# Second layer's up-projections: seven block products for eight on 20 of 22 pairs of hidden tiles

## The chip, the cores and the metric

The kernel runs on one core of a Trainium2 chip. The metric is device time in microseconds (us) of one execution, as the median of several runs. The engines are TensorE (PE in the profile; PEld is its weight load), VectorE (DVE), ScalarE (ACT), GpSimd (POOL) and SyncE (SP), which issues most transfers. Each engine works through its own list of instructions in a fixed order.

## The reference

Two layers of a hybrid backbone (neighbourhood attention and mLSTM in the first, latent attention in the second). What matters here is the gated feed-forward part, which both layers end in, in the second layer on 512 tokens:

```python
def conv_ffn(h, w_up, conv_w, conv_b, w_down):
    u = dwconv_centred(h @ w_up, conv_w, conv_b)
    a, g = jnp.split(u, 2, axis=-1)
    return (a * jax.nn.silu(g)) @ w_down
```

`h` is 512 x 1024, `w_up` 1024 x 5632 and `w_down` 2816 x 1024. The convolution has width 3 along the tokens. All is fp32, and the kernel holds fp32 accuracy by splitting each operand into a high and a low part (type fp32r) and taking three products: high x high, high x low, low x high.

## The kernel before

**Layout.** Activations lie as features x tokens: 8 blocks (k) of 128 features, 512 columns. The 2816 hidden features are 22 tiles of 128 (j). Each tile needs a pair of up-projection tiles: g = 0 is the value half, g = 1 the gate half. One up tile is 8 k x 3 products = 24 matmuls of 512 columns into one half of a two-bank PSUM tile `pu` (`proj`, L181).

**Weights.** `wload` (L175) fetches 128 x 1024 floats into `wraw` (a ring of two buffers), ScalarE copies the high part (`whi`), VectorE subtracts to get the low part (`wlo`). All of these small operations are recorded under the lines of the helpers: L139 matmul, L145 ScalarE, L148 two-input tensor operations, L154 VectorE's scalar-tensor-tensor.

**After the product** (`up_post`, L1214 on): ScalarE applies the middle tap and the bias of the convolution, two VectorE operations add the outer taps (straight from PSUM), ScalarE takes the SiLU of the gate, VectorE multiplies, ScalarE copies the high part of the hidden tile (`hid0`), VectorE subtracts the low part (`hid1`).

**Order.** The pairs come in groups (`plan`): here 3, 3, 3, 3, 3, 2, 1, 4. The first group is done in `front`, in two halves of 256 tokens, since the second half of `h` is finished late by the norm chain. For each further group the pairs' up-projections are written first and then, in `down`, the down-projection of the group before: 8 output tiles `pd`, each 3 matmuls per j of that group, added to `acc` by VectorE (by ScalarE copied for the first group). The last group's down-projection (`pdl`) runs in two halves of 256 tokens and feeds the last norm.

What stands in the program is the start only: a scheduler in the framework sets each engine's list, which is fixed when the kernel is built. Buffers are rings, and a writer waits until the last reader of its buffer is done.

## Time and profile before

| what | before |
|---|---|
| median of 3 runs | 1832.33 us (1832.32 to 1834.01) |
| profiled execution, its own time | 1829.64 us |
| span of the profile | 1827.5 us |
| PE busy | 1768.6 us (97%) |
| PEld / DVE / ACT / POOL busy | 1460.9 / 1162.9 / 748.5 / 254.6 us |
| granted TensorE clock, mean | 0.993 |

The feed-forward part of the second layer lies from about 1433 us to the end. Busy shares are averages over the whole program; the sections below read the stage itself. A matmul's own duration overlaps that of its neighbours, so the pace of TensorE is read from stretches: so many matmuls in so many us.

### The profile page before, as it was taken

How to read it: one execution, taken by the hardware profiler on the slowest of the kernel's cores; microseconds unless marked ns; L12 is line 12 of the kernel's file. 1: busy time of each engine (PE TensorE's matmuls, PEld its weight loads, DVE VectorE, ACT ScalarE, POOL GpSimd, SP SyncE). 2: the span in 40 equal slices, each digit the busy share in tenths (PEclk: the TensorE clock that was granted, in tenths of full speed). 3: DMA queues.
4: the chain of work that ended last, by engine and by line, in shares of the span. 5: the costliest groups of instructions: out<-in, count | busy, mean ns of one | idle time of the engine just before them, and what ended most of it. 6: DMA issues, size and time to landing. Idle time of an engine off the chain costs nothing.

```text
span 1827.5 us, 26602 instructions
## 1 busy us (share of the span) xinstructions
PE 1768.6 (97%) x10498; PEld 1460.9 (80%) x10498; DVE 1162.9 (64%) x2210; ACT 748.5 (41%) x1297; POOL 254.6 (14%) x306
## 2 busy tenths in 40 slices
PE   6999999999999999999999999899999999999997
PEld 4777787887778888888888877788878888888885
DVE  3383677557356686776764655788894574556565
ACT  3333444444444422232221334577775354333241
POOL 1000123234320000000000001344441200000000
PEclk8999999999999999999999999999999999999998
DMA  9343322214212343434421211000012132224231
GB/s 308 110 127 127 123 86 81 62 55 133 76 35 93 125 131 114 134 120 135 131 83 47 91 36 47 24 12 13 13 35 84 47 104 90 95 81 136 72 93 47
DMA packets 63261, 162.39 MB, mean 89 GB/s; under 512 B 6273, under 2 KB 19793, under 8 KB 63137
## 3 DMA queue, kind: packets, MB, share of 16 engines
q1 hardware_dynamic: 61616, 156.52, 27.0%
q0 software_dynamic: 1376, 4.04, 0.7%
q8 instruction: 83, 1.36, 0.3%
q14 instruction: 42, 0.34, 0.1%
q10 hardware_dynamic: 144, 0.13, 0.0%
HBM read 158.57 MB, written 2.10 MB: 88 GB/s over the span
## 4 chain that ended last, share of the span: by engine, by line
PE 84%; DVE 6%; POOL 2%; issue 2%; ACT 2%; DMA 1%; DVEq 0%; POOLq 0%; ACTq 0%
PE pu L139 29%; PE pd L139 13%; PE yps L139 4%; PE sp L139 4%; PE qkp L139 3%; PE puf L139 3%; PE pdl L139 3%; PE vtk L139 3%; PE qp L139 2%; PE pt L142 2%; PE ot L139 2%; PE vp L139 2%; PE kp L139 2%; PE ops L139 1%; PE ysum L390 1%
## 5 line engine op out<-in xcount | busy, mean ns | idle before, releaser
L145 ACT ACTIVATE whi<-wraw 128x1024 fp32r<-128x1024 f32 x186 | 195.2, 1058 | 484.8 <-PE pu L139 219.8
L148 DVE TENSOR_TENSOR wlo<-wraw,whi 128x1024 fp32r<-128x1024 f32 x184 | 224.7, 1226 | 236.4 <-ACT whi L145 235.8
L139 PE MATMUL pu<-h,whi 128*128 128x258 f32 (+1 forms) x1280 | 318.5, 339 | 0.0
L139 PEld LDWEIGHTS pu<-h,whi 128*128 128x128 f32 x1280 | 219.6, 188 | 28.7 <-issue 0.8
L139 PE MATMUL pd<-hid,whi 128*128 128x512 f32 (+1 forms) x864 | 233.4, 358 | 1.2 <-DVE acc L148 1.2
L139 PE MATMUL pu<-h,wlo 128*128 128x512 f32 (+1 forms) x640 | 216.6, 339 | 0.0
L139 PEld LDWEIGHTS pd<-hid,whi 128*128 128x128 f32 x864 | 152.2, 188 | 28.2 <-DVE acc L148 2.8
L148 POOL TENSOR_TENSOR ry<-rv,mhalf 128x2 f32<-128x2 f32 (+2 forms) x26 | 23.0, 884 | 1017.9 <-DVE rv L151 1017.9
L139 PE MATMUL pd<-hid,wlo 128*128 128x512 f32 (+1 forms) x432 | 153.1, 356 | 0.0
L148 DVE TENSOR_TENSOR acc<-pd,acc 128x512 f32<-128x512 f32 (+1 forms) x192 | 109.0, 585 | 47.9 <-PE pd L139 46.6
L139 PEld LDWEIGHTS pu<-h,wlo 128*128 128x128 f32 x640 | 120.9, 189 | 13.6
L139 PE MATMUL pu<-hb,whi 128*128 128x512 f32 x304 | 119.8, 394 | 0.0
L139 PE MATMUL pu<-hb,wlo 128*128 128x512 f32 x304 | 119.2, 392 | 0.0
L139 PE MATMUL pu<-lb,whi 128*128 128x512 f32 x304 | 118.0, 388 | 0.0
L154 DVE SCALAR_TENSOR_TENSOR av<-aw,s,av 128x512 f32<-128x512 f32 x140 | 102.5, 748 | 23.2 <-DMA aw<-in_ada_w_dram 22.6
L151 POOL TENSOR_SCALAR P<-P,rl 128x768 f32<-128x768 f32 (+1 forms) x96 | 85.3, 890 | 143.1 <-DVE nm L151 49.8
L139 PEld LDWEIGHTS pd<-hid,wlo 128*128 128x128 f32 x432 | 81.2, 188 | 11.9
L154 DVE SCALAR_TENSOR_TENSOR u<-pu,c_ffn_conv,u 128x769 f32<-128x769 f32 x80 | 81.1, 1014 | 10.1 <-ACT u L145 9.4
L139 PE MATMUL sp<-kr,qh 128*128 128x512 f32 (+1 forms) x256 | 71.0, 353 | 2.5 <-ACT P L145 1.3
L148 DVE TENSOR_TENSOR pTl<-pt,pTh 128x512 fp32r<-128x512 f32 x96 | 64.5, 682 | 5.7 <-ACT pTh L145 4.9
L139 PEld LDWEIGHTS pu<-hb,wlo 128*128 128x128 f32 x304 | 57.1, 188 | 13.4
L139 PEld LDWEIGHTS pu<-lb,whi 128*128 128x128 f32 x304 | 57.1, 188 | 12.7
(454 smaller groups left out, 3840.1 us busy)
## 6 DMA issues: line engine op xcount, KB each, us to landing
wraw<-in_ffn_up_dram SPq DMA_DIRECT2D x88, 512.0 KB, 3.6
aw<-in_ada_w_dram SPq DMA_DIRECT2D x112, 256.0 KB, 2.7
wraw<-in_ffn_down_dram SPq DMA_DIRECT2D x44, 512.0 KB, 3.6
aw<-in_ada_w_dram SPq DMA_DIRECT2D x40, 512.0 KB, 4.5
wraw<-in_w_in_dram SPq DMA_DIRECT2D x20, 512.0 KB, 3.7
wraw<-in_w_tok_dram SPq DMA_DIRECT2D x8, 512.0 KB, 4.2
wraw<-in_w_out_dram SPq DMA_DIRECT2D x8, 512.0 KB, 3.7
wraw<-in_w_o_dram SPq DMA_DIRECT2D x8, 512.0 KB, 3.5
```

The costliest lines, as they stand in the source:

```text
L139: PE.matmul(out=o, lhsT=l, rhs=r, start=start, stop=stop)
L142: PE.transpose(out=o, in_=i, identity=ident[0:i.shape[0], 0:i.shape[0]])
L145: S.activation(out=o, in_=i, func=func, **kw)
L148: e.tensor_tensor(out=o, in0=x, in1=y, op=op)
L151: e.tensor_scalar(out=o, in0=x, scalar1=s1, scalar2=s2, op0=op0, op1=op1)
L154: V.scalar_tensor_tensor(out=o, in0=x, scalar=s, in1=y, op0=op0, op1=op1)
L390: PE.matmul(out=ps[32 * i:32 * i + 32, 0:w], lhsT=ones32, rhs=src, start=first, stop=last, tile_position=(0, 32 * i))
```

## The change

The product of an up pair is seen as a 2 x 2 block product. The weights of a pair are four blocks: value or gate half (rows) by features k 0-3 or 4-7 (columns). The activations are four blocks: features 0-3 or 4-7 by the first or second 256 tokens. The direct way takes 8 block products, each 4 k x 3 = 12 matmuls of 256 columns; Strassen's scheme (in Winograd's form, with fewer additions) takes 7, at the price of sums: of activation blocks (T1 to T4, made once), of weight blocks (four per pair, on GpSimd) and of products.

This is done for the tiles j = 2 to 21. Per pair the new `up_s` has 7 products of 12 matmuls of 256 columns. Their results are put together in `c0`, `c1` in SBUF: ScalarE copies two of them, VectorE adds six times from PSUM, GpSimd adds once. The convolution then reads `c0`, `c1` from SBUF instead of PSUM. `weights(j)` is run one pair ahead, one step per product: it splits seven operands of 128 x 512 (w0 to w6, in `wq`, a ring of 8), with the four sums in between, made in place in `wraw`. On these pairs the gated multiply, the hidden low part and the low parts of the down weights go from VectorE to GpSimd. The groups become 2, 2, 2, 2, 1, 2, 2, 2, 2, 1, 4, so that eight down passes become eleven of fewer tiles, with the same matmuls in all. The norm chain ahead leaves `h` in fp32 in `acc` for the T sums, with one more ScalarE pass on six of eight feature blocks. The first layer is unchanged.

```diff
-                A, B, h = mod
+                A, B, h = mod[:3]
+                whole = len(mod) > 3
...
+                    elif whole:
+                        act(y(k), y(k), AF.Identity, bias=b)
+                        act(hi, y(k))
+                        tt(V, lo, y(k), fr(hi), ALU.subtract)
...
-            before_last=lambda: None, pumps=(0, 0), nst=NSF):
+            before_last=lambda: None, pumps=(0, 0), nst=NSF, blocks=None):
...
                 act(us[1], us[1], AF.Silu)
-                tt(V, us[0], us[0], us[1], ALU.mult)
+                eg = G if blocks else V
+                tt(eg, us[0], us[0], us[1], ALU.mult)
                 hi, lo = (t[:, c0:c0 + w] for t in hid[j])
                 act(hi, us[0])
-                tt(V, lo, us[0], fr(hi), ALU.subtract)
+                tt(eg, lo, us[0], fr(hi), ALU.subtract)
+            nh = n // 2
+            B, places, wst, nraw = {}, {}, {}, [0]
+            def blocks_ready(names):
+                h1_, h2_ = slice(0, nh), slice(nh, n)
+                a_ = lambda k0, c: acc[:, k0:k0 + 4, c]
+                t1, t3, t2, t4 = a_(0, h1_), a_(0, h2_), a_(4, h2_), a_(4, h1_)
+                for k0, c, nm in ((0, h1_, "11"), (4, h1_, "21"), (4, h2_, "22")):
+                    B[nm] = [lambda k, t=t, k0=k0, c=c: t[:, k0 + k, c] for t in h]
+                if "T4" in names:
+                    tt(G, t4, t4, t2, ALU.subtract)
+                else:
+                    tt(V, t1, t3, t1, ALU.subtract)
+                    tt(G, t3, t2, t3, ALU.subtract)
+                    tt(V, t2, t2, t1, ALU.subtract)
+                    places.update(blocks(fw))
+                for nm in names:
+                    t = {"T1": t1, "T2": t2, "T3": t3, "T4": t4}[nm]
+                    B[nm] = []
+                    for s in range(2):
+                        ps_ = places[nm][s]
+                        for k0, o in ps_:
+                            kn = o.shape[1]
+                            if s == 0:
+                                act(o, t[:, k0:k0 + kn])
+                            else:
+                                hi_ = [p for kk, p in places[nm][0] if kk <= k0][-1]
+                                kk_ = [kk for kk, p in places[nm][0] if kk <= k0][-1]
+                                tt(V, o, t[:, k0:k0 + kn], fr(hi_[:, k0 - kk_:k0 - kk_ + kn]), ALU.subtract)
+                        B[nm].append(lambda k, ps_=ps_: [o[:, k - k0] for k0, o in ps_
+                                                       if k0 <= k < k0 + o.shape[1]][0])
+            def block(o, w, b):
+                for k in range(4):
+                    wh, wl = (t[:, k * 128:(k + 1) * 128] for t in w)
+                    mm(o, wh, b[0](k), k == 0, False)
+                    mm(o, wh, b[1](k), False, False)
+                    mm(o, wl, b[0](k), False, k == 3)
+            def slot():
+                return fw.tile([128, 2, 512], F32R, tag="q", name="wq", bufs=8)
+            def raw_up(src):
+                nraw[0] += 1
+                p, tag = (wp, "wr") if nraw[0] % 4 < 2 else (fw, "raw")
+                raw = p.tile([128, 1024], F32, tag=tag, name="wraw", bufs=2)
+                nc.sync.dma_start(out=raw, in_=src)
+                return raw
+            def wunit(src, lo_e=None):
+                raw = raw_up(src)
+                hi, lo = (slot().rearrange("p a b -> p (a b)") for _ in range(2))
+                act(hi, raw)
+                tt(lo_e or V, lo, raw, fr(hi), ALU.subtract)
+                return hi, lo
+            def weights(j):
+                ra, rg = (raw_up(a["ffn_up"][l, 2 * j + g]) for g in range(2))
+                w = wst[j] = []
+                a11, a12, a21, a22 = ra[:, 0:512], ra[:, 512:1024], rg[:, 0:512], rg[:, 512:1024]
+                for i, r in enumerate((a11, a22, a12, a11, a21, a22, a12)):
+                    hi, lo = (lambda t: (t[:, 0], t[:, 1]))(slot())
+                    act(hi, r)
+                    tt(V, lo, r, fr(hi), ALU.subtract)
+                    w.append((hi, lo))
+                    if i == 1:
+                        tt(G, a22, a21, a22, ALU.add)
+                        tt(G, a21, a11, a21, ALU.subtract)
+                        tt(G, a11, a22, a11, ALU.subtract)
+                    elif i == 2:
+                        tt(G, a12, a12, a11, ALU.subtract)
+                    yield
+            def up_s(j, early):
+                w = wst.pop(j)
+                nxt = weights(j + 1) if j + 1 < NH else iter(())
+                C = [fw.tile([128, pw], F32, tag=f"c{g}", name=f"c{g}") for g in range(2)]
+                c11, c12, c21, c22 = (c[:, o:o + nh] for c in C for o in (0, nh))
+                us = [None, None]
+                def conv(g):
+                    u = us[g] = fw.tile([128, pw], F32, tag=f"u{g}", name=f"u{g}", bufs=1)
+                    cw = fcw[l][:, g * NH + j, :]
+                    act(u, C[g], AF.Identity, scale=cw[:, 1:2], bias=cw[:, 3:4])
+                    stt(u[:, 1:n], C[g][:, 0:n - 1], cw[:, 0:1], u[:, 1:n], ALU.mult, ALU.add)
+                    stt(u[:, 0:n - 1], C[g][:, 1:n], cw[:, 2:3], u[:, 0:n - 1], ALU.mult, ALU.add)
+                for i, (m, nm) in enumerate([(0, "11"), (1, "T4"), (2, "21"), (3, "T2"), (4, "T3"), (5, "T1"), (6, "22")]
+                                            if not early else
+                                            [(0, "11"), (2, "21"), (3, "T2"), (4, "T3"), (5, "T1"), (6, "22"), (1, "T4")]):
+                    if i % 2 == 0:
+                        pa = ps_a("pu")
+                    p = pa[:, 512 * (i % 2):512 * (i % 2) + nh]
+                    block(p, w[m], B[nm])
+                    if m == 0:
+                        act(c12, p)
+                    elif m == 1:
+                        if early:
+                            tt(V, c21, p, c21, ALU.add)
+                        else:
+                            act(c21, p)
+                    elif m == 2:
+                        tt(V, c11, p, c12, ALU.add)
+                    elif m == 3:
+                        tt(V, c12, p, c12, ALU.add)
+                    elif m == 4:
+                        if early:
+                            tt(V, c21, p, c12, ALU.add)
+                        else:
+                            tt(V, c22, p, c12, ALU.add)
+                            tt(G, c21, c21, c22, ALU.add)
+                    elif m == 5:
+                        tt(V, c22, p, c21 if early else c22, ALU.add)
+                        tt(V, c12, p, c12, ALU.add)
+                    else:
+                        tt(V, c12, p, c12, ALU.add)
+                    next(nxt, None)
+                    if m == (1 if early else 5):
+                        conv(1)
+                conv(0)
+                run(nxt)
+                gated(j, us, 0, pw)
             def up(j):
+                if blocks:
+                    return up_s(j, j == plan[1][0])
...
-                wus = {j: [wload(a["ffn_up"][l, 2 * j + g],
+                wus = {j: [wunit(a["ffn_up"][l, 2 * j + g]) if blocks and 2 * n_ + g >= 3 else
+                           wload(a["ffn_up"][l, 2 * j + g],
...
+                        if blocks and sg is parts[-1][-1]:
+                            blocks_ready(("T2", "T3", "T1"))
...
-                wu = {j: (wload(a["ffn_down"][l, j], tag="wd", pool=fw, bufs=gmax) if n_ < gmax
+                wu = {j: ((wload(a["ffn_down"][l, j], lo_e=G) if n_ < 3 else wunit(a["ffn_down"][l, j], G)) if blocks
+                          else wload(a["ffn_down"][l, j], tag="wd", pool=fw, bufs=gmax) if n_ < gmax
...
+            if blocks:
+                blocks_ready(("T4",))
+                run(weights(plan[1][0]))
...
+                    elif blocks and i == 0:
+                        for _ in range(KD // 2):
                             next(dn, None)
...
-    out_proj(a["w_o"], h1, acc1, SH, xs1, mods1["G1"], tuple(range(KD)), (mods1["A2"], mod_shift(1, 3), h1), NSO[1],
+    out_proj(a["w_o"], h1, acc1, SH, xs1, mods1["G1"], tuple(range(KD)), (mods1["A2"], mod_shift(1, 3), h1, True),
+             NSO[1],
...
-    ffn(1, SH, SH, [SH], xs1, h1, accp, acc1, mods1["G2"], [3] * 5 + [2, 1, 4], done=emit_out)
+    def blocks1(fw):
+        v = vkp.tile([128, 6, TX], F32R, tag="v1", name="tb", bufs=2).rearrange("p a b -> p (a b)")
+        f = fw.tile([128, 3, TX * 2], F32R, name="tb2", bufs=1)
+        fl = lambda t: t.rearrange("p (a b) -> p a b", a=4)
+        return {"T2": [[(0, fl(v[:, 0:1024]))], [(0, fl(v[:, 1024:2048]))]],
+                "T3": [[(0, fl(v[:, 2048:3072]))], [(0, fl(f[:, 0]))]],
+                "T1": [[(0, fl(f[:, 1]))], [(0, fl(f[:, 2]))]],
+                "T4": [[(0, hb1[:, 0:4, 256:512])], [(k, h1lo[k][:, 256:512].unsqueeze(1)) for k in range(4)]]}
+    ffn(1, SH, SH, [SH], xs1, h1, accp, acc1, mods1["G2"], [2] * 4 + [1] + [2] * 4 + [1, 4], done=emit_out,
+        blocks=blocks1)
```

**How the instructions move, 1: VectorE.** In the middle of the second layer's feed-forward part, one pair before: the outer taps from `pu`, the low parts of later weights, the multiply and the low hidden part.

```order
L154 SCALAR_TENSOR_TENSOR u0_15627<-pu_15565,fcw1_13268,u0_15627 128x511 x2
L148 TENSOR_TENSOR wlo_15732<-wraw_15729,whi_15731 128x1024
L154 SCALAR_TENSOR_TENSOR u1_15631<-pu_15596,fcw1_13268,u1_15631 128x511
L148 TENSOR_TENSOR wlo_15827<-wraw_15824,whi_15826 128x1024
L148 TENSOR_TENSOR u0_15627<-u0_15627,u1_15631 128x512
L148 TENSOR_TENSOR hid1_15636<-u0_15627,hid0_15635 128x512
```

In the change, the second pair of a group, from the fourth weight operand (w3) of the pair to come to the first tap of the value half:

```order
L148 TENSOR_TENSOR wq_14773<-wraw_14716,wq_14773 128x512
L148 TENSOR_TENSOR c0_14700<-pu_14742,c0_14700 128x256
L148 TENSOR_TENSOR c1_14701<-pu_14776,c0_14700 128x256
L148 TENSOR_TENSOR wq_14791<-wraw_14718,wq_14791 128x512
L148 TENSOR_TENSOR wq_14808<-wraw_14718,wq_14808 128x512
L148 TENSOR_TENSOR c1_14701<-pu_14776,c1_14701 128x256
L148 TENSOR_TENSOR c0_14700<-pu_14776,c0_14700 128x256
L148 TENSOR_TENSOR wq_14829<-wraw_14716,wq_14829 128x512
L154 SCALAR_TENSOR_TENSOR u1_14811<-c1_14701,fcw1_13268,u1_14811 128x511
L148 TENSOR_TENSOR c0_14700<-pu_14815,c0_14700 128x256
L148 TENSOR_TENSOR acc1_13270<-pd_14842,acc1_13270 128x512
L154 SCALAR_TENSOR_TENSOR u0_14832<-c0_14700,fcw1_13268,u0_14832 128x511
```

The taps now read two operands in SBUF, the multiply and the low hidden part are gone from this list, and the split w3 (first row) stands ahead of the additions from PSUM and of the taps.

**2: GpSimd.** Before, nothing stands between the last norm work ahead of the pairs and the first of the last norm:

```order
L151 TENSOR_SCALAR acc1_13270<-acc1_13270,mod1_102 128x256 [waits DVE_49]
L148 TENSOR_TENSOR lb2_12992<-acc1_13270,hb_12846 128x256 [waits PE_49,Activation_49]
L148 TENSOR_TENSOR lb5_13139<-acc1_13270,hb_12846 128x256 [waits PE_49,Activation_49]
L148 TENSOR_TENSOR ry_16508<-rv_16507,mhalf_90 128x2 [waits DVE_49]
L148 TENSOR_TENSOR x1_4390<-acc1_13270,x1_4390 128x256 [waits DVE_49] x2
```

In the change, from the end of a group's first pair to the start of the next group's (`wlo` are down weights; `u0` is the multiply, `hid1` the low hidden part, `wraw` the four sums, `c1` the addition of two products):

```order
L148 TENSOR_TENSOR wlo_14667<-wraw_14664,whi_14666 128x1024 [waits DMAHW2_49,PE_49,Activation_49]
L148 TENSOR_TENSOR u0_14654<-u0_14654,u1_14633 128x512 [waits DVE_49,Activation_49]
L148 TENSOR_TENSOR wlo_14673<-wraw_14670,whi_14672 128x1024 [waits DMAHW3_49,PE_49,Activation_49]
L148 TENSOR_TENSOR hid1_14659<-u0_14654,hid0_14658 128x512 [waits Activation_49]
L148 TENSOR_TENSOR wraw_14718<-wraw_14718 128x512 [waits DMAHW1_49,DVE_49]
L148 TENSOR_TENSOR wraw_14718<-wraw_14716,wraw_14718 128x512 [waits DMAHW0_49,Pool_49]
L148 TENSOR_TENSOR wraw_14716<-wraw_14718,wraw_14716 128x512 [waits Pool_49]
L148 TENSOR_TENSOR wraw_14716<-wraw_14716 128x512 [waits DVE_49,Pool_49]
L148 TENSOR_TENSOR c1_14701<-c1_14701 128x256 [waits DVE_49]
L148 TENSOR_TENSOR u0_14832<-u0_14832,u1_14811 128x512 [waits DVE_49,Activation_49]
L148 TENSOR_TENSOR hid1_14837<-u0_14832,hid0_14836 128x512 [waits PE_49,Activation_49]
```

The multiply and the low hidden part of a pair stand ahead of the sums for the weights that are split during the next pair.

**3: ScalarE.** In the change, behind a group's second pair: the first product of the next pair (`c0` from `pu_14884`) stands ahead of the second weight operand, w1 (`wq_14918`), and the second product ahead of the next ones.

```order
L145 ACTIVATE u1_14811<-u1_14811 128x512
L145 ACTIVATE hid0_14836<-u0_14832 128x512
L145 ACTIVATE c0_14882<-pu_14884 128x256
L145 ACTIVATE wq_14918<-wraw_14900 128x512
L145 ACTIVATE c1_14883<-pu_14884 128x256
L145 ACTIVATE wq_14938<-wraw_14898 128x512
L145 ACTIVATE wq_14955<-wraw_14898 128x512
```

Before, ScalarE's list there held copies of whole weight tiles between the middle taps:

```order
L145 ACTIVATE u0_15627<-pu_15565,fcw1_13268 128x512
L145 ACTIVATE whi_15731<-wraw_15729 128x1024
L145 ACTIVATE u1_15631<-pu_15596,fcw1_13268 128x512
L145 ACTIVATE whi_15826<-wraw_15824 128x1024
L145 ACTIVATE u1_15631<-u1_15631 128x512
L145 ACTIVATE hid0_15635<-u0_15627 128x512
```

So a weight copy that waited for a transfer alone before now also stands behind products of TensorE.

More of the change, by code (lines that the diff above doesn't have):

```diff
@@ L1216, in up_post @@
                     pu = pus[g]
-                    u = fw.tile([128, pw], F32, tag=f"u{g}", name=f"u{g}")[:, c0:c0 + w]
+                    u = fw.tile([128, pw], F32, tag=f"{'c' if blocks else 'u'}{g}", name=f"u{g}")[:, c0:c0 + w]
                     cw = fcw[l][:, g * NH + j, :]
@@ L1222, in up_post, with gated @@
                     us.append(u)
+                gated(j, us, c0, w)
+            def gated(j, us, c0, w):
                 if j not in hid:
-                    hid[j] = [fw.tile([128, pw], F32R, tag=f"u{i}", name=f"hid{i}") if j == NH - 1 else
-                              fw.tile([128, pw], F32R, tag=f"hid{i}", name=f"hid{i}", bufs=2 * gmax) for i in range(2)]
+                    hid[j] = [fw.tile([128, pw], F32R, tag=f"{'c' if blocks else 'u'}{i}", name=f"hid{i}") if j == NH - 1
+                              else fw.tile([128, pw], F32R, tag=f"hid{i}", name=f"hid{i}", bufs=2 * gmax)
+                              for i in range(2)]
@@ L1321, in ffn @@
                     before_last()
-                    lastp = fs.enter_context(tc.tile_pool(name=f"fl{l}", bufs=1, side="right", reuse_waits="tile"))
+                    lastp = None if blocks else fs.enter_context(tc.tile_pool(name=f"fl{l}", bufs=1, side="right", reuse_waits="tile"))
                 dn = down(gi, js)
@@ L1327, in ffn @@
                         for _ in range(INS[l][i]):
+                            next(dn, None)
+                    elif blocks and i == 0:
+                        for _ in range(KD // 2):
                             next(dn, None)
@@ L1582, in hybrid_backbone_kernel @@
                     ts(G, d_[64:128, :], fr(s_[64:128, :]), 1.0, 0.0, ALU.mult, ALU.add)
-        h1hi, h1lo = [], []
+        h1hi, h1lo, hbs = [], [], []
         def split_mix(k):
@@ L1589, in split_mix @@
                 h1hi.extend(t[:, i, :] for i in range(6))
+                hbs.append(t)
             elif k > 5:
@@ L1655, in emit_out @@
         nc.sync.dma_start(out=out[k * 128:(k + 1) * 128, sg.po:sg.po + sg.w], in_=xs1[sg](k))
-    ffn(1, SH, SH, [SH], xs1, h1, accp, acc1, mods1["G2"], [3] * 5 + [2, 1, 4], done=emit_out)
+    hb1 = hbs[0]
+    def blocks1(fw):
[8 more added lines that the diff above has]
+        blocks=blocks1)
     until(SH[1])
```

## The prediction

> **What bounds the kernel now.** I read the chain of waits first, then busy time by stage, then groups by shape. The chain in the second layer's feed-forward part (start us, us, what):
>
> ```profile
> 1452.65 0.40 PE bcm L142 x2
> 1453.06 22.38 PE puf L139 x190
> 1475.44 32.97 PE pu L139 x144
> 1508.41 16.37 PE pd L139 x72
> ...
> 1786.80 4.55 PE pdl L139 x36
> ```
>
> From the last norm broadcast (`bcm`) on, nothing but TensorE is on the chain. It gives the paces: a matmul of 256 columns takes 22.38 / 190 = 0.118 us, one of 512 columns 32.97 / 144 = 0.229 us, in `pd` 16.37 / 72 = 0.227. A group of three pairs takes 49.3 us, a pair 16.45. Busy time in one such stretch (PE, PEld, DVE, ACT, POOL, clock, DMA):
>
> ```profile
> 1524.80:1574.10 49.30, 49.30 (x217) 40.51 (x217) 27.91 (x34) 17.76 (x22) 0.00 (x0) 1.00 0.31 97
> ```
>
> TensorE never stops, VectorE works 57% of the time, GpSimd not at all. So a matmul removed is worth its time for as long as the other engines keep up: that is the question here. The sum is made against the profiled execution's own 1829.64 us, 0.15% below the median of 1832.33.
>
> **What the change takes from TensorE.** Before: 288 matmuls of 256 columns in `front`, 912 of 512 in `pu`: 288 x 0.118 + 912 x 0.229 = 242.8 us. After: 192 in `front` and 20 x 7 x 12 = 1680, all of 256: 1872 x 0.118 = 220.9. That is 22 us less; the down matmuls stay. Per pair: 84 x 0.118 = 9.9 us of products and 24 x 0.227 = 5.45 of down, so 15.35.
>
> `front` loses 11.3 us of this, but its matmuls covered the end of the norm chain: behind `bcm` the order had 46 matmuls that need no new `h`, now 9. 37 x 0.118 = 4.4 us lie open.
>
> **What it adds elsewhere.** The rows to cost it by (xcount | busy us, mean ns):
>
> ```profile
> L148 POOL TENSOR_TENSOR ql<-q,qh 128x512 fp32r<-128x512 f32 x16 | 20.8, 1298 | 1.0
> L148 POOL TENSOR_TENSOR x<-acc,x 128x256 f32<-128x256 f32 x14 | 12.1, 862 | 21.2 <-DVE acc L154 21.2
> L148 POOL TENSOR_TENSOR wlo<-wraw,whi 128x1024 fp32r<-128x1024 f32 x2 | 5.1, 2555 | 19.3 <-ACT whi L145 19.3
> ...
> L154 DVE SCALAR_TENSOR_TENSOR u<-pu,fcw,u 128x511 f32<-128x511 f32 x76 | 56.8, 747 | 10.9 <-ACT u L145 9.6
> L148 DVE TENSOR_TENSOR acc<-pd,acc 128x512 f32<-128x512 f32 x48 | 32.5, 686 | 24.1 <-PE pd L139 24.1
> L148 DVE TENSOR_TENSOR hid<-u,hid 128x512 fp32r<-128x512 f32 x22 | 15.1, 689 | 6.0 <-ACT hid L145 5.6
> L148 DVE TENSOR_TENSOR acc<-pdl,acc 128x256 f32<-128x256 f32 x16 | 6.7, 421 | 13.4 <-PE pdl L139 13.4
> ...
> L145 ACT ACTIVATE whi<-wraw 128x1024 fp32r<-128x1024 f32 x62 | 64.9, 1057 | 139.0 <-PE pu L139 69.4 <-DMA wraw<-in_ffn_up_dram 27.1 <-DMA wraw<-in_ffn_down_dram 19.5
> L145 ACT ACTIVATE hid<-u 128x512 fp32r<-128x512 f32 x22 | 13.8, 629 | 12.2 <-DVE u L148 12.1
> L145 ACT ACTIVATE srow<-ysum 128x256 f32<-128x256 f32 x3 | 1.2, 385 | 3.7 <-PE ysum L390 3.7
> ...
> wraw<-in_ffn_down_dram SPq DMA_DIRECT2D x44, 512.0 KB, 3.6
> ```
>
> A pair costs GpSimd six operations of 512 (four sums, the multiply, the low hidden part), one of 256 and one down low part: 6 x 1.30 + 0.86 + 2.55 = 11.2 us. It costs VectorE seven splits, four taps, six additions from PSUM and four to `acc`. VectorE issues its next operation 0.09 us before a span ends (`x` at 1442.61 for 0.42, the next at 1442.94, below), so that a split or an `acc` addition costs 0.60, a tap 0.66, an addition of 256 0.33: 4.2 + 2.64 + 2.0 + 2.4 = 11.2. ScalarE: nine passes of 0.63 beside the two of the hidden tile, two of 0.39 and one of 1.06, about 9 us. Each alone is below 15.35. By sums of busy time TensorE would still be the bound.
>
> **The order says otherwise.** GpSimd's list has, in this order, the multiply M and low part H of one pair, then the sums S1 to S3; the split w3 needs S3, and on VectorE w3 stands ahead of the next pair's taps; M of the next pair needs these taps. This closes a ring that each pair passes once, with GpSimd and VectorE at work one after the other. Its legs:
>
> *VectorE's leg*, from w3 to the end of the value half's taps: w3 0.60, addition from the fourth product 0.33. That addition frees the PSUM bank of the last product, five of whose matmuls stand ahead of the sixth product's twelve: 17 x 0.118 = 2.0 us, in which w4, w5 and the GpSimd addition pass. Then two additions 0.66, w6 0.60, tap 0.66, addition 0.33, tap 0.66: 5.84. In a group's first pair w0 and the last two taps follow (0.60 + 0.66 + 0.75): 7.85. In its second pair two `acc` additions stand between them: 8.45.
>
> *GpSimd's leg after a first pair.* The two down low parts stand before M and before H. The first one's transfer waits for a buffer that w6 frees, 3.66 us before the taps end; landing 3.6, ScalarE 1.06 and GpSimd 2.55 put its end 3.55 us behind the taps. Then M 1.30, the second one 2.55, H 1.30, S1 to S3 3.90, ScalarE 0.63: 13.2. With VectorE's 8.45 that is 21.7 us.
>
> *After a second pair.* S1 needs w1 split, w1's high part stands on ScalarE behind the copy of the next pair's first product, and TensorE has 30 down matmuls before that product: 30 x 0.227 + 1.41 = 8.2 us from the last product, which ends 4.7 us before the taps do (2.61 + 0.66 + 0.33 for what VectorE does from its addition on, 1.1 for its wait on that addition). So S1 starts at 3.5 + 0.39 + 0.63 + 0.69 = 5.2; S1 to S3 3.9, ScalarE 0.63, VectorE 7.85: 17.6.
>
> Both exceed 15.35, and their mean exceeds the 16.45 of before. No row shows such a ring; its members are all rows.
>
> **The shared input.** GpSimd and VectorE hold each other up where both read two operands from SBUF (start us, us; GpSimd first):
>
> ```profile
> 459.15 1.35 POOL L148 TENSOR_TENSOR ysq<-ysq 128x512 f32<-128x512 f32 x1 [3.63 <-ACT ysq L145]
> 461.12 1.61 POOL L148 TENSOR_TENSOR ysq<-ysq 128x512 f32<-128x512 f32 x1 [0.62 <-ACT ysq L145]
> ...
> 1441.64 1.99 POOL L148 TENSOR_TENSOR x<-acc,x 128x256 f32<-128x256 f32 x1 [0.27 <-DVE acc L154]
> ```
>
> ```profile
> 458.12 1.23 DVE L148 TENSOR_TENSOR wlo<-wraw,whi 128x1024 fp32r<-128x1024 f32 x1 [3.83 <-ACT whi L145]
> 460.04 1.55 DVE L148 TENSOR_TENSOR wlo<-wraw,whi 128x1024 fp32r<-128x1024 f32 x1 [0.69 <-ACT whi L145]
> ...
> 1441.47 1.22 DVE L148 TENSOR_TENSOR wlo<-wraw,whi 128x1024 fp32r<-128x1024 f32 x1
> 1442.61 0.42 DVE L148 TENSOR_TENSOR x<-acc,x 128x256 f32<-128x256 f32 x1
> 1442.94 0.87 DVE L154 SCALAR_TENSOR_TENSOR acc<-acc,G,bcy 128x256 f32<-128x256 f32 x2
> ```
>
> GpSimd's 0.86 became 1.99: it began 0.6 us after VectorE's `x` had ended, and not beside. VectorE's 1.23 became 1.55 behind GpSimd's end at 460.50, and GpSimd's 1.30 became 1.61 behind VectorE's at 461.59. In the ring this costs a pair between 0 (each finds a gap) and 1.3 us: 0.6 where w2's split falls between the sums, 0.67 where S4 (1.30, behind S3) outlasts ScalarE's 0.63 and holds w3 up. I take 0.65, the middle, since both rows above show waits, but in a stretch with fewer operations than here.
>
> The Trainium skill states this ("SBUF — State Buffer", section "Who interferes with whom"): a VectorE instruction with two SBUF inputs and a GpSimd instruction that reads SBUF exclude each other for a whole instruction. The rows above agree. What it makes of the taps, now with both inputs in SBUF, is a rival below.
>
> **The sum.** From the end of `front` to the last down-projection there are 19 rounds: 8 behind a first pair with two down low parts, 22.35; 2 with one, 19.8; 7 behind a second pair, 18.25; the last 2, where the sums partly stand ahead of H, 5 x 1.30 + 0.63 + 7.85 + 0.65 = 15.65. That is 178.8 + 39.6 + 127.8 + 31.3 = 377.5. The first pair adds 12 (9.9 of products and 2 of taps), the end M, ScalarE, H and a last low part, 5.8. In all 395 us, against 1786.8 - 1475.4 = 311.4: 84 more. `front` gives 11.3 - 4.4 = 6.9 back. 1829.64 + 84 - 7 = **1907 us**, 4% slower. Bounds of the shared input alone: 12 us either way. The T sums (four of 1024) lie beside `front` and its post-processing; I take them at nothing, and if that cover is gone they cost two GpSimd operations, 5 us.
>
> **Rivals.**
>
> *TensorE stays the bound (faster).* Weights are made a pair ahead, and each engine has less than 15.35 us of work per pair. If the framework's order let the legs overlap, the time would be 1829.64 - 22 + 4.4 = 1812. Against it: lists are fixed, and the ring's barest passage, M 1.30, ScalarE 0.63, H and three sums 5.2, ScalarE 0.63 and VectorE 7.85, is 15.6, just above TensorE's. It decides if the ring is under 15.35. Chance 0.10.
>
> *The ring holds, but without the down weights' and w1's waits* (transfers early, products early): rounds of 15.6 to 16.2 plus 0 to 1.3. With 16.5: 19 x 16.5 + 18 - 311 - 7 = 13, so 1843; from 1829 to 1858. For it: transfers land in 3.6 us and TensorE has slack once it waits. Chance 0.14, of which 0.04 within 0.2% (3.7 us, about what a measurement here tells from no change).
>
> *The shared input alone sets the pace.* Spans of GpSimd, 11.2, and VectorE's two-operand work, 4.2 + 2.64 = 6.8, add to 18.0 per pair if neither ever overlaps: 19 x 18 + 18 - 311 - 7 = 42, so 1871. For it: the rows above. Against it: the ring's mean, 19.9, is longer. Chance 0.13, from 1858 to 1880.
>
> *Full serialization*: besides, VectorE's other work (4.4) and ScalarE's two passes (1.26) lie open: 23.7 per pair, so 450 + 18 - 311 - 7 = 150 and 1980. Against it: in the ring GpSimd and VectorE do overlap at w0 to w2. Chance 0.07.
>
> The forecast, 1880 to 1955, holds 0.56. That the change saves no matmuls is excluded: its list has 1680 of 256 columns.
>
> **Numbers.** The range 1838 to 1958 leaves out the first rival, a part of the second and the last: 0.20. Faster 0.10, within 0.2% 0.04, slower 0.86.
>
> **What would show it.** Right: `pu` waits for VectorE or ScalarE in every pair; GpSimd's list runs M, H, sums without a gap while VectorE waits for ScalarE's `wq`; rounds of about 22 and 18 us in turn, PE busy about 75% in this part; GpSimd spans beyond 1.30. Wrong: TensorE unbroken with 84 matmuls in 9.9 us per pair (first rival), or rounds equal within a group (no wait for the down weights).

## The result, and the profile after

The changed kernel takes 1951.38 us in the median of four runs (1950.22 to 1953.16), against 1832.32 before: a ratio of 1.0648, 95% interval 1.0634 to 1.0661. It is 6.5% slower. The forecast was 1907, in a range of 1838 to 1958; its direction holds, its size is 44 us too small, and the time lies 7 us inside the upper end of the range.

The same stage as in the prediction's second quotation, now over 300 us (PE, PEld, DVE, ACT, POOL, clock, DMA):

```profile
1500.00:1800.00 300.00, 241.35 (x1477) 215.62 (x1478) 196.30 (x283) 116.88 (x199) 168.92 (x113) 0.93 0.25 74
```

TensorE, unbroken before, is busy for 80% of the time, VectorE for 65%, GpSimd for 56%, and the granted clock is no longer 1.00. No engine is full. Who waits for whom between 1500 and 1860 us (engine, line, releaser: us in total, times, longest):

```profile
ACT wq L145 <- POOL wraw L148: 80.8, 16, 8.5
DVE wq L148 <- ACT wq L145: 75.3, 30, 4.7
POOL u L148 <- DVE u L154: 65.8, 10, 7.9
...
PE pu L139 <- DVE c L148: 42.9, 26, 4.0
```

This is the ring: the split of a sum waits for GpSimd's sums, VectorE for that split, GpSimd's multiply for VectorE's taps, TensorE for VectorE's additions. One round behind a first pair, GpSimd and then VectorE (start us, us):

```profile
1541.07 2.71 POOL L148 TENSOR_TENSOR wlo<-wraw,whi 128x1024 fp32r<-128x1024 f32 x1 [5.40 <-PE pu L139]
1543.74 1.29 POOL L148 TENSOR_TENSOR u<-u,u 128x512 f32<-128x512 f32 x1
1544.98 2.37 POOL L148 TENSOR_TENSOR wlo<-wraw,whi 128x1024 fp32r<-128x1024 f32 x1
1547.31 1.75 POOL L148 TENSOR_TENSOR hid<-u,hid 128x512 fp32r<-128x512 f32 x1
1549.01 5.70 POOL L148 TENSOR_TENSOR wraw<-wraw 128x512 f32<-128x512 f32 x4
```

```profile
1554.07 1.20 DVE L148 TENSOR_TENSOR wq<-wraw,wq 128x512 fp32r<-128x512 f32 x1 [1.84 <-ACT wq L145]
1555.18 0.94 DVE L148 TENSOR_TENSOR c<-pu,c 128x256 f32<-128x256 f32 x2
1556.04 1.81 DVE L148 TENSOR_TENSOR wq<-wraw,wq 128x512 fp32r<-128x512 f32 x2
1558.98 0.76 DVE L148 TENSOR_TENSOR c<-pu,c 128x256 f32<-128x256 f32 x2 [1.12 <-PE pu L139]
...
1563.87 0.74 DVE L154 SCALAR_TENSOR_TENSOR u<-c,fcw,u 128x511 f32<-128x511 f32 x1
```

The last taps of the pair before ended at 1541.56. GpSimd then runs the first down low part, the multiply M, the second low part, H and the four sums without a gap, and VectorE starts w3 at 1554.07 and ends its taps at 1564.61: a GpSimd leg of 12.5 us (13.2 predicted) and a VectorE leg of 10.5 (8.45 predicted). A round behind a second pair (taps ending at 1522.26 and 1541.56):

```profile
1522.40 1.29 POOL L148 TENSOR_TENSOR u<-u,u 128x512 f32<-128x512 f32 x1 [5.97 <-DVE u L154]
1524.43 1.29 POOL L148 TENSOR_TENSOR hid<-u,hid 128x512 fp32r<-128x512 f32 x1 [0.74 <-ACT hid L145]
1527.34 5.72 POOL L148 TENSOR_TENSOR wraw<-wraw 128x512 f32<-128x512 f32 x4 [1.62 <-DVE wq L148]
```

S1 starts 5.1 us behind the taps (5.2 predicted), and the round takes 19.3 (18.25). From taps to taps, worked out from the end of each pair's last tap, the first ten rounds take 23.0, 19.3, 23.0, 19.9, 22.1, 19.3, 26.8, 21.7, 21.2, 19.4; all 19 take 405.3 us, against 377.5 predicted.

### The profile page after: what moved, and what is told of

Its sections match the earlier page's. It is cut to its first block, busy times and chain, and to the rows that moved or that the text cites. A ratio compares the mean times of both kernels' runs of the same rounds, so it can differ in the third digit from the quotient of the medians.

```text
span 1951.3 us, 28688 instructions
## 1 busy us (share of the span) xinstructions
PE 1799.0 (92%) x11170; PEld 1511.3 (77%) x11170; DVE 1268.4 (65%) x2398; ACT 808.1 (41%) x1452; POOL 507.1 (26%) x473
## 4 chain that ended last, share of the span: by engine, by line
PE 69%; DVE 10%; POOL 9%; issue 6%; ACT 3%; DMA 2%; POOLq 0%; DVEq 0%; ACTq 0%; SPq 0%
PE pu L139 22%; PE pd L139 9%; POOL wraw L148 4%; PE yps L139 4%; PE sp L139 4%; PE qkp L139 3%; PE pdl L139 3%; PE vtk L139 3%; PE qp L139 2%; PE pt L142 2%; PE ot L139 2%; PE vp L139 2%; DVE u L154 2%; PE kp L139 2%; PE puf L139 2%
## 5 line engine op out<-in xcount | busy, mean ns | idle before, releaser
L145 ACT ACTIVATE whi<-wraw 128x1024 fp32r<-128x1024 f32 x144 | 151.4, 1057 | 350.1 <-PE pu L139 150.5
L148 DVE TENSOR_TENSOR wlo<-wraw,whi 128x1024 fp32r<-128x1024 f32 x121 | 148.2, 1228 | 151.5 <-ACT whi L145 151.3
L148 DVE TENSOR_TENSOR wq<-wraw,wq 128x512 fp32r<-128x512 f32 (+1 forms) x141 | 140.4, 1012 | 95.8 <-ACT wq L145 87.1
L139 PE MATMUL pu<-hb,wq 128*128 128x256 f32 x640 | 137.5, 301 | 45.9 <-DVE c L148 30.4
L139 PEld LDWEIGHTS pu<-hb,wq 128*128 128x128 f32 x640 | 110.8, 203 | 56.7 <-DVE c L148 35.9
L145 ACT ACTIVATE wq<-wraw 128x512 fp32r<-128x512 f32 (+1 forms) x142 | 86.2, 629 | 162.3 <-POOL wraw L148 90.1
L139 PE MATMUL pu<-tb,wq 128*128 128x256 f32 x720 | 113.0, 316 | 27.0 <-DVE c L148 25.2
L139 PEld LDWEIGHTS pu<-tb,wq 128*128 128x128 f32 x720 | 105.1, 221 | 31.5 <-DVE c L148 29.1
L148 POOL TENSOR_TENSOR wraw<-wraw 128x512 f32<-128x512 f32 x80 | 110.6, 1383 | 20.8 <-DVE wq L148 16.7
L139 PE MATMUL pu<-lb,wq 128*128 128x256 f32 x320 | 93.4, 294 | 0.0
```

The lines of the kernel that those rows point to most:

```text
L139: PE.matmul(out=o, lhsT=l, rhs=r, start=start, stop=stop)
L145: S.activation(out=o, in_=i, func=func, **kw)
L148: e.tensor_tensor(out=o, in0=x, in1=y, op=op)
```

## The experiments

"Rounds" below is the sum of these 19 rounds in the profiled run. All times are medians; the kernel before took 1832 to 1835 us beside them.

### M and H, the down low parts, and both, back on VectorE; no weight late

```diff
-                eg = G if blocks else V
+                eg = V
```

> The gated multiply M and the low hidden part H go back to VectorE; GpSimd keeps the sums, the product addition and the low parts of the down weights. Ring theory: M no longer ties the sums to the taps, but the first down low part still waits for the buffer that w6 frees, and both stand ahead of S1. From w6 on: transfer 3.6, ScalarE 1.06, two low parts 5.1, S1 to S3 3.9, ScalarE 0.63, w3 to w6 4.2, so 18.5 us after a first pair, and about 18 after a second one (the wait of S1 for w1 is not touched). VectorE gets 1.2 us more. 19 rounds sum to about 345 by durations taken alone; the change measured 405 where such a sum gave 377, so 345 to 370, and 1951 - 405 + 345 to 370 = 1891 to 1916 us. Shared input alone: 2.6 us less on GpSimd and 1.2 more on VectorE, 1.4 per pair, so 1951 - 27 = 1924. TensorE or the start as the cause: 1951, no difference.

```diff
-wload(a["ffn_down"][l, j], lo_e=G) if n_ < 3 else wunit(a["ffn_down"][l, j], G)
+wload(a["ffn_down"][l, j]) if n_ < 3 else wunit(a["ffn_down"][l, j])
```

> The low parts of the down weights go back to VectorE; GpSimd keeps M, H, the sums and the product addition. Ring theory: a round after a first pair becomes M 1.3, ScalarE 0.63, H and S1 to S3 5.2, ScalarE 0.63, VectorE 8.45 and one split of 1.14 more, with 0.65 for the shared input, 18.0 us; one after a second pair stays near 18.3. The rounds become equal: 19 x 18.1 = 344 by durations taken alone, to 370 as measured, so 1890 to 1916 us. Shared input alone: 2.55 less on GpSimd and 1.14 more on VectorE, so 1951 - 27 = 1924. TensorE or the start as the cause: 1951.

Both edits together:

> M, H and the low parts of the down weights all go back to VectorE; GpSimd has the four sums and one addition of 256. VectorE then has 11.2 + 1.2 + 1.14 = 13.5 us per pair. Ring theory: the ring is open, since GpSimd waits for nothing that comes behind the taps. What is left is within a pair: from the end of its first product, copy 0.39, w1's high part 0.63 and low part 0.69, S1 to S3 3.9, ScalarE 0.63, w3 0.6, addition 0.33, 17 matmuls 2.0, in all 9.2 us against the 8.5 of 72 matmuls, so a round of 1.4 + 9.2 + 5.45 = 16.0: 19 x 16.0 = 304, 1951 - 405 + 304 = 1850 us, 1838 (TensorE's 15.35) to 1880 (7% more as measured). Both edits together then bring more than the sum of the one and the other could without a ring. Shared input alone: 1951 - 53 = 1898. Start as the cause: 1951.

```diff
                 for i, r in enumerate((a11, a22, a12, a11, a21, a22, a12)):
+                    if i > 1:
+                        w.append(w[i % 2])
+                        yield
+                        continue
...
-                        tt(G, a22, a21, a22, ALU.add)
-                        tt(G, a21, a11, a21, ALU.subtract)
-                        tt(G, a11, a22, a11, ALU.subtract)
...
-                        tt(G, a12, a12, a11, ALU.subtract)
```

> Only w0 and w1 are split and the other five products reuse them; the four weight sums are left out too, so the up-projections of these 20 pairs come out of the wrong weights. All matmuls, additions, taps, M, H and down low parts stay. It shows what the 84 matmuls per pair take when no weight is late. Ring theory: the ring is cut at the sums, TensorE's 15.35 us per pair are the bound: 19 x 15.35 = 292, so 1951 - 405 + 292 = 1838 us, up to 1850 if GpSimd's M, H and low parts hold the gate. If the pace of the matmuls of 256 columns, their banks or the taps' own chain were the cause, rounds stay above 18 us and the time above 1890.

| kernel | us | ratio to before | rounds |
|---|---|---|---|
| changed | 1951.4 | 1.0648 [1.0634, 1.0661] | 405.3 |
| M, H on VectorE | 1933.1 | 1.0551 [1.0535, 1.0567] | 386.0 |
| down low parts on VectorE | 1925.1 | 1.0504 [1.0488, 1.0519] | 378.1 |
| both | 1915.9 | 1.0459 [1.0442, 1.0477] | 370.6 |
| two splits, no sums | 1857.8 | 1.0141 [1.0126, 1.0156] | 312.3 |

Each edit helps although it hands work to the busier engine, and with the down low parts gone the first ten rounds are nearly equal (18.6 to 20.8, one of 24.3), as the ring has it. But all three gains are smaller than the ring theory's. The shared input as the only cause had 1924, 1924 and 1898 us for the three: the second is met (1925), the first and the third are not. With both, GpSimd waits for nothing behind the taps, and yet the rounds are 19.5 on the mean where 16.0 was expected: 1916 is above the ring's 1850 and even above the shared input's 1898. The last row shows that matmuls, banks and taps aren't it: with weights never late the rounds are 16.4. So something beside the ring holds the weights.

### The sums without their dependence, two idle additions, no T sums, filled pauses

Beside these four runs the kernel before took 1834.6 us, 2.3 more than beside the changed kernel; differences of a few us to the changed kernel are given by the ratios as well.

```diff
-                        tt(G, a22, a21, a22, ALU.add)
-                        tt(G, a21, a11, a21, ALU.subtract)
+                        tt(G, jk, a21, a22, ALU.add)
+                        tt(G, jk, a11, a21, ALU.subtract)
...
```

> The four weight sums are still computed on GpSimd, at their places in its list and from the same inputs, but into a spare tile that nobody reads; the splits take the unsummed weights, so the up-projections of these 20 pairs come out of the wrong weights. GpSimd and VectorE have the work that they had, on the same inputs; only the dependence of w3 to w6 on the sums is gone. Ring theory: the ring is cut, rounds fall from the 21.3 of the change to about the 16.4 that the kernel with two splits showed, plus what seven splits leave open: 16.4 to 17.5, so 1951 - 405 + 312 to 333 = 1858 to 1879 us. Shared input as the pace (spans of GpSimd and of VectorE's two-operand work end to end, 18.0 by durations and more as measured): no difference, 1930 to 1951.

1941.5 us (1.0576 [1.0560, 1.0592]), rounds 391.5: 10 us less than the changed kernel (13 by the ratios), where the ring theory had 72 to 93. The prediction's edge from the sums to w3 is worth little by itself here. The run is not a clean cut, though: the sums no longer wait for w1, two of them move ahead of M in GpSimd's list, and ScalarE's copy of H's high part, which needs M, stands ahead of the copy of the next pair's first product in ScalarE's list, so that a second ring can take over: in the trace ScalarE's copy of H's high part waits 65.6 us for M between 1500 and 1860 us, against 37.4 in the changed kernel.

```diff
                     if m == (1 if early else 5):
+                        if not early:
+                            for _ in range(2):
+                                jk = fw.tile([128, nh], F32, tag="jk", name="jk", bufs=1)
+                                tt(G, jk, c21, c21, ALU.add)
                         conv(1)
```

> Two more GpSimd additions of 128x256 per pair, on 19 of the 20 pairs, 0.86 us each, into a spare tile, right behind the addition of the products: there GpSimd's list is idle until the taps are done, and VectorE works through w6 and the four taps. Nobody waits for their result. Shared input between GpSimd and VectorE: each holds up one of the five two-operand operations of VectorE's leg, which is on the ring: 0.4 to 0.9 us each, so 19 x 0.8 to 1.7 = +15 to +32, 1966 to 1983 us. No shared input: 1951, no difference.

1951.1 us (1.0640 [1.0624, 1.0655]): no difference, against the shared input's +15 to +32. The place of the two additions suggests why (one pair; GpSimd, then VectorE):

```profile
1534.21 1.11 POOL L148 TENSOR_TENSOR c<-c 128x256 f32<-128x256 f32 x1 [1.49 <-DVE c L148]
1535.40 1.64 POOL L148 TENSOR_TENSOR jk<-c 128x256 f32<-128x256 f32 x2
```

```profile
1536.06 0.76 DVE L148 TENSOR_TENSOR c<-pu,c 128x256 f32<-128x256 f32 x2 [0.18 <-PE pu L139]
1536.73 0.86 DVE L148 TENSOR_TENSOR wq<-wraw,wq 128x512 fp32r<-128x512 f32 x1
```

They pass for the most part while VectorE adds from PSUM, which has one operand in SBUF, and the split behind them is late by 0.17 us. Over all pairs between 1500 and 1860 us VectorE's splits take 1.07 us on the mean (1.06 in the changed kernel) and its taps 0.78 in both. So here a GpSimd operation without two-operand work of VectorE beside it cost nothing.

```diff
-                    tt(V, t1, t3, t1, ALU.subtract)
-                    tt(G, t3, t2, t3, ALU.subtract)
-                    tt(V, t2, t2, t1, ALU.subtract)
...
+                    B[nm] = B["12"] if nm != "T4" else B["11"]
```

> The sums of activation blocks T1 to T4 and their splits are left out; the products that used them take blocks of h as they are, so the up-projections of these 20 pairs come out wrong. From the last product of the front to the first taps the change took 27.2 us where the prediction had 12, with a gap of TensorE ahead of the first product. If the T sums stand on that path: 1951 - 13 to - 17, so 1934 to 1938 us. If they are hidden, as predicted, or cost their two GpSimd operations: 1946 to 1951. The rounds behind the first pair should stay at 405 in sum either way.

1946.1 us (1.0604 [1.0587, 1.0622]): 5.3 us less (8 by the ratios), near the price of the two GpSimd operations and not 13 to 17. But it is not these operations. In the changed kernel three splits of T sums stand on VectorE ahead of the last taps of `front`, and TensorE's first product waits for one of these taps (VectorE, then TensorE):

```profile
1466.40 5.70 DVE L148 TENSOR_TENSOR tb<-acc,tb 128x1024 fp32r<-128x1024 f32 x3
```

```profile
1477.48 0.55 PE L139 MATMUL pu<-hb,wq 128*128 128x256 f32 x1 [5.47 <-DVE u L154]
```

Without the T sums that wait is 1.15 us, and the taps of the first pair end at 1492.5 instead of 1499.2. The rest of the late start is elsewhere.

```diff
                     block(p, w[m], B[nm])
+                    if not early and i == 4:
+                        for k in range(16):
+                            mm(pa[:, 256:512], h[0][:, 0, 0:128], h[0][:, k % 4, 0:256], True, True)
```

> On 19 of the 20 pairs 16 more matmuls of 256 columns (1.9 us) on blocks of h stand behind the fifth product's, where TensorE waits 2.4 us in most rounds, and write to PSUM columns that nobody reads. If the halves of the granted clock come from these pauses and lie on the path: fewer of the 18 halved windows of 3.4 us between 1500 and 1900 us, and 1.7 us less for each that goes: 10 of them give 1951 - 17 = 1934 us. If the halved clock costs nothing, or does not come from the pauses: 1951, or later by what the matmuls take where TensorE didn't wait, up to 7 rounds x 1.9 = 13, 1964.

1971.4 us (1.0748 [1.0732, 1.0764]): 20 us more, later than either reading had it. Halved time between 1500 and 1880 us fell from 54.6 to 34.1 us by the clock's records, six windows, while 304 more matmuls (36 us at 0.118) were run. So filling pauses took halved windows away, but what a halved window costs can't be taken from this run; the trace of the changed kernel tells more (below).

### The shared input, measured: sums nobody waits for, no sums, sums on VectorE

All three start from the kernel with M, H and the down low parts on VectorE (1915.9 us). The first has the sums into a spare tile as above, the second leaves the four sums out, the third is

```diff
-                        tt(G, a22, a21, a22, ALU.add)
-                        tt(G, a21, a11, a21, ALU.subtract)
-                        tt(G, a11, a22, a11, ALU.subtract)
+                        tt(V, a22, a21, a22, ALU.add)
+                        tt(V, a21, a11, a21, ALU.subtract)
+                        tt(V, a11, a22, a11, ALU.subtract)
```

> M, H and the down low parts on VectorE, and the four weight sums computed on GpSimd into a spare tile that nobody reads; the splits take the unsummed weights, so the up-projections of these 20 pairs come out of the wrong weights. It has the work of the kernel with M, H and the down low parts on VectorE (1916 us, rounds of 19.5 on the mean), without the wait of w3 to w6 for the sums. If these rounds are the leg that the prediction gave for a round after a second pair (w1, S1 to S3, w3, VectorE's leg): they fall to 16.4 to 17, 1916 - 371 + 312 to 323 = 1857 to 1868 us. If they are the shared input or VectorE's 13.5 us of work with its waits: 1905 to 1916.

> The same with the four sums left out altogether (wrong weights as well): GpSimd keeps one addition of 256 per pair. Its difference to the kernel with the sums into a spare tile is what the sums cost by GpSimd's presence on the shared input, without any dependence. With the input shared: 19 x 1 to 2 = 20 to 40 us less than that kernel. Without: equal. If VectorE's list alone sets the rounds, it stays near 1900.

> M, H, the down low parts and the sums S1 to S3 on VectorE; GpSimd keeps S4 and one addition of 256 per pair. The result is the reference's. VectorE has 13.5 + 1.8 = 15.3 us per pair, and S1 to S3 take 1.8 instead of 3.9 (4.35 as measured), with no change of engine between w1 and S1. If the leg from w1 to w3 sets the rounds: 19.5 - 2.5 = 17.0, 1916 - 371 + 323 = 1868 us. If VectorE's work sets them: 19.5 + 1.8 = 21.3, 1950 us.

| kernel | us | ratio to before | rounds |
|---|---|---|---|
| sums on GpSimd, waited for | 1915.9 | 1.0459 [1.0442, 1.0477] | 370.6 |
| sums on GpSimd, nobody waits | 1901.3 | 1.0383 [1.0365, 1.0400] | 352.3 |
| no sums | 1844.2 | 1.0066 [1.0051, 1.0081] | 300.7 |
| S1 to S3 on VectorE | 1864.1 | 1.0173 [1.0158, 1.0188] | 319.7 |

The dependence on the sums is worth 15 us, their mere presence on GpSimd 57. That the sums keep their inputs' buffers longer is not the cause: with sums that nobody waits for, ScalarE's copies for the splits waited only 1.4 us in all for transfers between 1500 and 1830 us. VectorE's groups between 1500 and 1830 us (busy us, mean ns, idle before) with sums that nobody waits for, and then without sums:

```profile
L148 DVE TENSOR_TENSOR wq<-wraw,wq 128x512 fp32r<-128x512 f32 x120 | 108.1, 918 | 4.6 <-PE pu L139 2.7 <-ACT wq L145 1.9
L154 DVE SCALAR_TENSOR_TENSOR u<-c,fcw,u 128x511 f32<-128x511 f32 x69 | 59.3, 860 | 0.4
...
L148 DVE TENSOR_TENSOR c<-pu,c 128x256 f32<-128x256 f32 x103 | 41.7, 419 | 36.1 <-PE pu L139 23.3 <-POOL c L148 11.6
L148 DVE TENSOR_TENSOR wlo<-wraw,whi 128x1024 fp32r<-128x1024 f32 x16 | 20.0, 1254 | 2.0 <-ACT whi L145 2.0
L148 DVE TENSOR_TENSOR hid<-u,hid 128x512 fp32r<-128x512 f32 x18 | 18.0, 1002 | 1.4 <-ACT hid L145 1.4
L148 DVE TENSOR_TENSOR u<-u,u 128x512 f32<-128x512 f32 x18 | 17.4, 966 | 0.1
```

```profile
L148 DVE TENSOR_TENSOR wq<-wraw,wq 128x512 fp32r<-128x512 f32 x123 | 86.5, 719 | 10.4 <-ACT wq L145 5.3 <-PE pu L139 5.1
L154 DVE SCALAR_TENSOR_TENSOR u<-c,fcw,u 128x511 f32<-128x511 f32 x76 | 56.6, 746 | 0.4
...
L148 DVE TENSOR_TENSOR c<-pu,c 128x256 f32<-128x256 f32 x113 | 45.9, 420 | 21.0 <-PE pu L139 19.3
L148 DVE TENSOR_TENSOR wlo<-wraw,whi 128x1024 fp32r<-128x1024 f32 x19 | 23.6, 1249 | 2.2 <-ACT whi L145 2.2
L148 DVE TENSOR_TENSOR hid<-u,hid 128x512 fp32r<-128x512 f32 x19 | 13.0, 686 | 0.8 <-ACT hid L145 0.7
L148 DVE TENSOR_TENSOR u<-u,u 128x512 f32<-128x512 f32 x19 | 13.0, 684 | 0.1
```

Splits, taps, M and H, which have both operands in SBUF, are longer; the additions from PSUM stay at 0.42. The low parts of the down weights have both operands in SBUF too and stay at 1.25, so two operands alone aren't enough: the sums have to run beside the operation. Per pair: 7 x 0.199 + 4 x 0.114 + 0.316 + 0.282 = 2.45 us, and 11.6 / 17 = 0.7 of waiting for GpSimd's product addition, which stands behind the sums: 3.1, against 2.7 per round measured ((352.3 - 300.7) / 19). The 57 us also hold what follows from this: between 1500 and 1800 us the granted clock was halved for 27.3 us with these sums and for 0.4 us without them, and no run takes the two apart. How it looks in sequence, GpSimd and VectorE of the kernel with sums that nobody waits for:

```profile
1597.26 4.97 POOL L148 TENSOR_TENSOR jk<-wraw 128x512 bf16<-128x512 f32 x3
```

```profile
1597.65 0.68 DVE L148 TENSOR_TENSOR acc<-pd,acc 128x512 f32<-128x512 f32 x1
1598.25 1.16 DVE L148 TENSOR_TENSOR wq<-wraw,wq 128x512 fp32r<-128x512 f32 x1
1599.33 1.77 DVE L148 TENSOR_TENSOR hid<-u,hid 128x512 fp32r<-128x512 f32 x1
1601.03 2.35 DVE L148 TENSOR_TENSOR wq<-wraw,wq 128x512 fp32r<-128x512 f32 x2
```

The three sums start at 1597.26, 1598.94 and 1600.63, and the two engines take turns: the first split, H and the next split each last as long as the rest of GpSimd's operation and about 0.55 us of their own; the last split, with no sum beside it, takes 0.68. With S1 to S3 on VectorE, which then has 15.3 us of work per pair, the time is 52 us lower than with them on GpSimd, and VectorE is busy for 96% of the time:

```profile
1500.00:1800.00 300.00, 282.51 (x1888) 252.84 (x1887) 288.73 (x471) 148.28 (x251) 42.80 (x36) 0.99 0.27 88
```

### The sums alone moved

The diff of the last table's last row, made on the changed kernel itself:

> One edit on the changed kernel: S1 to S3 on VectorE instead of GpSimd, 1.8 us more per pair there. M, H, the down low parts, S4 and the product addition stay on GpSimd, in the old order. The result is the reference's. If the cost of the change lies in the sums on GpSimd (waited for by w3, and holding up VectorE's splits at the shared input): VectorE has 13.0 us per pair, GpSimd's list is left with a leg of 3.55 + 1.3 + 2.55 + 1.3 + 1.3 + 1.1 = 11.1 behind a first pair's taps and VectorE's 5 from there on, 16.1; rounds of 16.5 to 17.5, 1951 - 405 + 313 to 333 = 1859 to 1879 us. If M, H and the down low parts on GpSimd cost what they did beside the sums (36 us): 1864 + 36 = 1900. If VectorE's list is the bound whatever stands on GpSimd: 1951 + 19 x 1.8 = 1985.

1911.6 us (1.0427 [1.0408, 1.0445]), rounds 365.6: 40 us less, but far from 1859 to 1879. Beside sums that cost little, M, H and the down low parts on GpSimd still cost 1911.6 - 1864.1 = 48 us. How much of this is the shared input and how much the waits for M, H and the one sum left on GpSimd stays open. One of them, and the tap that meets it:

```profile
1578.19 2.38 POOL L148 TENSOR_TENSOR wlo<-wraw,whi 128x1024 fp32r<-128x1024 f32 x1 [4.35 <-ACT whi L145]
```

```profile
1578.85 2.27 DVE L154 SCALAR_TENSOR_TENSOR u<-c,fcw,u 128x511 f32<-128x511 f32 x1 [0.54 <-ACT u L145]
```

A tap of 0.75 takes 2.27 and ends 0.55 us after the low part does. The edits bring a little more together than apart: -36 for M, H and low parts, -40 for S1 to S3, -87 for all of it, which is 9.0 us of GpSimd work per pair turned into 4.1 of VectorE's by the prediction's prices. None of these kernels beats the one before (the best that computes the reference is the 1864.1 one).

## Why the prediction was right, and where it wasn't

**What held.** TensorE is no longer the bound, as the forecast had it against its first rival; GpSimd's list runs without a gap while VectorE waits for ScalarE's `wq`, and long and short rounds alternate until the tenth; behind that the long one follows the second pair, since there the list has the down low parts elsewhere. The GpSimd leg (12.5 for 13.2) and the start of S1 (5.1 for 5.2) came out of the rows of before. In the GpSimd leg two errors cancel in part, which is luck: the first low part ended 2.2 us behind the taps and not 3.55, and H (1.75) and the sums (1.43 each) took longer than 1.30.

**A step that was mis-sized is the shared input.** It stood in the sum with 0.65 us per pair, between 0 and 1.3, from two places of the old trace where the engines met seldom. (One of these rows was misread: GpSimd's 1.99 us from 1441.64 end 0.6 us after VectorE's `x` has ended; it did not begin there.) Taken by itself in a kernel without the ring it is 2.7 per round, the clock's part included. In the changed kernel splits take 1.06 us on the mean and taps 0.78 between 1500 and 1860 us, against 0.72 and 0.75 in the kernel without sums: 7 x 0.34 + 4 x 0.03 = 2.5 us per pair, of which a part only lies on the ring. In 16 of the 19 rounds w3 took 1.20 to 1.22 behind S4; w4 and w5 took 1.81 together beside the product addition, but that is hidden, since VectorE then waits for TensorE.

**A term that the sum did not have is the granted clock.** On VectorE's leg stand 17 matmuls, taken at 2.0 us. In the long round above they took 3.2, most of them at half clock, and VectorE waited 1.12 us for them (the row at 1558.98). In the short round before it, at full clock, it waited 0.18:

```profile
1536.40 0.76 DVE L148 TENSOR_TENSOR c<-pu,c 128x256 f32<-128x256 f32 x2 [0.18 <-PE pu L139]
```

In 11 of the 19 rounds a halved stretch lies over this wait, and it is 0.76 to 1.58 us long; in five, at full clock, it is 0.18 or 0.19; in the other three the order is another. That is 12 us of the 27.8 that the rounds are over. The other 16, or 0.8 per round, fit the shared input, which would then have cost about 1.5 and not 0.65 per round; no run measures this remainder by itself.

The prediction had the shared input as a rival of its own too, with 18.0 us per pair and 1871 as the time. Ring and shared input aren't alternatives: taking away either of them alone made the kernel faster. That one limit lies just below the other fits the cuts of the ring, each of which brought less than it promised (-18, -26, -36 for -35 to -60, -35 to -61 and -71 to -113); with M and H on VectorE and the sums still on GpSimd, M and H took 1.32 and 1.38 us there, against 0.68 and 0.69 without sums. The second rival's rounds of 16.5, the ring without two of its waits, were not reached: no run with the four sums on GpSimd came below 18.5 (352.3 / 19).

The Trainium skill has the rule ("SBUF — State Buffer", section "Who interferes with whom"): the engines' shared ports are an exclusive lock, held for a whole instruction, and a VectorE instruction contends for them when it has two SBUF inputs. The tap of 2.27 us agrees, and so do the additions from PSUM, unchanged at 0.42. The prediction quoted it and then priced it by rows with too few meetings.

**Where the 47 us between 1907 and the profiled time went.** Rounds +27.8 (405.3 for 377.5). First pair +15.2: 27.2 us from the end of `front` (1472.0) to its taps (1499.2), for 12. Three stretches of it:

```profile
1472.00:1477.50 5.50, 0.03 (x2) 0.05 (x1) 5.50 (x12) 2.62 (x5) 0.00 (x0) 0.74 0.00 0
1477.50:1481.00 3.50, 2.87 (x12) 2.58 (x12) 3.22 (x6) 2.54 (x4) 1.51 (x1) 0.50 0.36 80
1481.00:1485.00 4.00, 1.60 (x7) 1.60 (x8) 1.91 (x2) 2.01 (x4) 2.71 (x3) 0.50 0.51 197
```

TensorE stands still for 5.5 us, then runs at half clock. Of the 15, the T sums are 5 to 8, by the run without them. The prediction took them at nothing, and at 5 us if their cover was gone; that this number is near is luck, since it stood for two GpSimd operations, and what TensorE waited for were taps of `front` behind VectorE's splits of the T sums. For the rest there is only the trace: GpSimd's list has M and H of both pairs of `front` among the first sums, from 1479.41 to 1491.96, so that the ring's leg stands in the first pair too. `front` itself ended 3.4 us earlier than before and not 6.9 (+3.5). The end came as predicted: the long run of `pdl` matmuls that begins at 1786.80 before begins here 5.9 us behind the last taps (1904.49), where the prediction had 5.8, and from there it is 40.9 us to the end, 40.7 before.

```profile
1910.36 4.46 PE pdl L139 x35
```

Together 46.8.

## What to carry to other kernels

An engine that shows as idle isn't free if it shares its way into SBUF with the one that it relieves: here 9.0 us of GpSimd work per pair, off VectorE at 4.1, cost 87 us with the waits that it brought, and the four sums cost 57 where nobody waited for them. A price for that is taken where the two engines are both dense, not where they meet once. When work moves between in-order engines, follow one turn through all lists and then ask which second limit lies just below it, since undoing one edge of a ring gives back no more than the distance to that limit. Where an experiment takes a dependence away, leave the work in place, and in a second one take the work away: the difference of the two (15 and 57 us) is the answer.
